# Strassen's seven products in all four feed-forwards of a decoder trunk, six direct pairs each, and the hybrid mixer's weights cut on arrival

## The chip, the cores and the metric

The kernel runs on one core of a Trainium2 chip. The metric is the device time of one execution in microseconds (us). The runs of one kernel differ by about 0.1%. One more execution is taken with the hardware profiler on; its page and its trace are what is quoted here.

## The reference, cut to what matters

The input is 512 tokens of width 1024 in float32. There are two layers; each is

```
x = x + 0.5 * ffn1(norm(x));  x = x + mixer(norm(x));  x = x + 0.5 * ffn2(norm(x))

def swiglu_ffn(x, g, w_in, w_out):            # w_in 1024 x 5632, w_out 2816 x 1024
    h = rms_norm(x, g)
    gate, up = jnp.split(h @ w_in, 2, axis=-1)
    return (jax.nn.silu(gate) * up) @ w_out
```

The mixer of layer 0 (hybrid) projects to seven parts of 512 columns: gate, q, k and v of eight retention heads, and q, k and v of eight heads of dilated window attention; the 1024 columns that come out go through an output projection. The mixer of layer 1 is stick-breaking attention with 16 heads. A last norm ends it. Everything is float32, and the kernel keeps about that accuracy on TensorE with three products for one: each operand is split into a rounded high part (hi) and the rest (lo), and hi*hi + hi*lo + lo*hi is accumulated.

## The kernel before, in words

**Data.** Activations are transposed: x is eight tiles x0 to x7 of 128 channels x 512 tokens that stay in SBUF. All large tiles come from 43 slots of 4 KB a partition. `give` (line 49) hands lists of slots to roles, and `B` (line 72) takes the next slot of a role in turn. The roles for weights are `wraw` (four slots, a weight as it comes from HBM) and `whl` (six slots, so three pairs of hi and lo). The Tile framework orders each engine's instructions from priorities and a model of their times and adds the semaphores; engines work through their queues in order. Inside mixers and the feed-forwards of `ffn_seven`, the order on TensorE is the order in the source (`ordered`, line 113).

**Weights, four ways.**

- `weight` (line 144): load raw, hi by a cast on ScalarE (line 206), lo by a subtraction on VectorE (line 207).
- `cut_ahead` (line 175) does this early, beside other work, and writes hi and lo to HBM with two transfers; `weight_cut` (line 185) later reads both, and no engine has to work on them.
- `weight_dma` (line 481): load raw, hi by a cast and minus hi by a multiplication on ScalarE (lines 485 and 486), then POOL issues a transfer that reads the weight from HBM again and adds it onto minus hi (line 487), which gives lo without VectorE.
- `centre` (line 162) is for the retention's v: the mean over each head's 64 columns is taken out on VectorE (lines 168 and 169), and the result goes to HBM.

**Feed-forwards.** There are 22 tiles of 128 gate columns and 22 of up columns. A direct pair is one of each: a tile is 8 x 3 matmuls of 512 columns (tokens). The first feed-forward of layer 0 (`ffn`, line 388) has 22 direct pairs; beside them it centres the four v weights and cuts 20 weights of the hybrid mixer ahead. The other three (`ffn_seven`, line 538) have four direct pairs and then nine quads. A quad (line 490) is two pairs done at once as a 2 x 2 product of blocks (rows are the halves of the 1024 channels, columns the two column groups; tokens are split in halves of 256) with seven products instead of eight, in Winograd's form of Strassen's method. It loads four raw blocks, makes four sums of blocks on VectorE, and cuts seven operands: four sums with `cut_form` (ScalarE and VectorE), three raw blocks with `cut_raw` (line 456, ScalarE twice and an accumulating transfer from POOL, line 461). A product is 24 matmuls of 256 columns. The other operand, seven combinations of the normed activations with hi and lo, is made once a feed-forward (`normed_forms`, line 430; lines 440 to 452), after the last direct pair in the source, and as early as VectorE comes to it. Three of the eight direct weights are cut with `weight_dma` (`BYDMA`, line 427). The quads have seven slots for raw blocks and ten for cut ones. At the end all 22 tiles of silu(gate) * up are split into hi and lo (line 580).

**Output projection.** `out_ffn` (line 300) does eight tiles of 22 x 3 matmuls in three pieces of weights each, adds half of the result to x, and makes the next norm's h (gain times x, split, line 231) and the sum of squares (line 240) for each tile as it comes. Beside it `cut_ahead` runs 12 times (first feed-forward of layer 0: eight hybrid weights, four of the stick mixer), 16 times and 16 times. The factor 1/rms (`norm_r`, line 262) is applied after the first projections.

**Hybrid mixer** (line 835). The 28 units of input weights (four gates, four each of rq, rk, dq and dk, and four each of rv and dv) are used in a fixed stream of steps. All were cut ahead; `weight_cut` takes turns between the `wraw` and the `whl` slots. First come the four gates, q and k of the first head pair and values, then steps are interleaved with the heads: scores, masks by POOL (line 777) or softmax, values. Then the output projection, whose last three chunks are done by `out_second` (line 372).

Of the kernel before, what the change touches and what calls it, by code (L numbers as in the profile page):

```python
# [20 lines left out]
P = 128  # L21
# [8 lines left out]
NORM_EPS = 1e-6  # L30
GN_EPS = 1e-5


@with_exitstack
def trunk(ctx: ExitStack, tc: tile.TileContext, a: dict, out: bass.AP):
# [17 lines left out]
    give(wraw=WSLOTS[:4], whl=WSLOTS[4:])  # L53
    home = {"h": list(range(10, 18))}

    def others():

        return [i for i in range(10, NSLOT) if i not in home["h"]]
# [116 lines left out]
    def cut_ahead(key, cols):  # L175

        hi, lo = weight(centred.get(key, array_unit(key)), cols)
        keep = dram.tile([P, 2, cols], F32, tag="cut_" + "_".join(map(str, key)), name="cut_" + "_".join(map(str, key)))
        for i, part in enumerate((hi, lo)):
            nc.sync.dma_start(keep[:, i, :], f32(part[:, :cols]))  # L180
        cut[key] = keep

    turns = [0]
# [10 lines left out]
    def unit(key, cols):  # L194
        if key in cut:
            return weight_cut(key, cols)
        return weight(array_unit(key), cols)

# [41 lines left out]
    def norm_sum(c, ss, sl=slice(0, SEQ)):  # L240
        if c == 0:
            nc.scalar.activation(out=ss[:, sl], in_=x[c][:, sl], func=AF.Square)
        else:
            s = T()[:, sl]
            nc.scalar.activation(out=s, in_=x[c][:, sl], func=AF.Square)
            nc.vector.tensor_add(out=ss[:, sl], in0=ss[:, sl], in1=s)

    def norm_chunk(c, gcol, ss):
        norm_h(c, gcol)
        norm_sum(c, ss)  # L250

# [9 lines left out]

    def norm_r(ss, epsr=None):
        ps = PS("po")
        mm(ps, ones_ms, ss, start=True, stop=True)
        r = rstd(ps, NORM_EPS, eps_n, "r")
        if epsr is not None:
            nc.vector.tensor_scalar(out=epsr, in0=ps, scalar1=NORM_EPS, scalar2=GN_EPS, op0=ALU.add, op1=ALU.mult)
        return r
# [31 lines left out]
    def out_ffn(w_out, us, gcol, ahead, n):  # L300

        ss = norm_start()
        act_set(LNEXP)
        for d in range(KC):
            ps = ACC()
            m = n * (d + 1) // KC - n * d // KC
            out_tile(w_out[d], ps, us, then=lambda p: cut_ahead(*ahead.pop(0)) if p in (8, 15)[2 - m:] else None)
            add_half(d, ps)
            norm_chunk(d, gcol, ss)
        return ss  # L310
# [61 lines left out]
    def out_second(wb, chunks, gcol):  # L372

        ss = norm_start()
        for d0 in range(0, KC, 4):
            ws = [unit((wb, d0 // 2 + i), 768) for i in range(2)]
            ps = [ATT() for _ in range(4)]
            for f in ((0, 1), (2,)):
                for i in range(4):
                    for g in f:  # L380
                        mm3(ps[i], ws[i // 2], (i % 2) * 384 + g * P, chunks[5 + g][:, 0, :], chunks[5 + g][:, 1, :],
                            g == 0, g == 2)
            for i in range(4):
                nc.vector.tensor_add(out=x[d0 + i], in0=ps[i], in1=x[d0 + i])
                norm_chunk(d0 + i, gcol, ss)
        return ss

    def ffn(r, w_in, first=None, ahead=None, extra={}):

        us = []  # L390
        give(u=others()[:FC])
        for f in range(FC):
            pg = ACC()
            if first and f == 0:
                pu = ATT()
                for k in range(KC):
                    for w, ps in zip(first, (pg, pu)):
                        mm3(ps, w, k * P, hh[k][:, 0, :], hh[k][:, 1, :], k == 0, k == KC - 1)
            else:
                proj_tile(w_in[f], pg)  # L400
            if f == 0:
                rr = r()
                act_set(SILU)
            t1 = T(tag="tp")
            nc.vector.tensor_mul(out=t1, in0=pg, in1=rr)
            s = T()
            func(s, t1, AF.Silu)
            if not (first and f == 0):
                pu = ATT()
                proj_tile(w_in[FC + f], pu)  # L410
            t2 = T(tag="tp")
            nc.vector.tensor_mul(out=t2, in0=pu, in1=rr)
            nc.vector.tensor_mul(out=t2, in0=t2, in1=s)
            u = B((P, 2, SEQ), F32R, "u")
            split(u[:, 0, :], u[:, 1, :], t2)
            us.append(u)
            if ahead and f > 1:
                if f in extra:
                    centre(extra[f])
                cut_ahead(*ahead.pop(0))  # L420
        return us

    DIRECT, FORMS_AT = 4, 3
    FIRST, BYDMA = 40, (5, 6, 7)
    HT = SEQ // 2
# [51 lines left out]

    def weight_dma(src, cols):
        raw = B((P, 1024), F32, "wraw")
        hi, lo = (B((P, 1024), F32R, "whl")[:, :cols] for _ in range(2))
        nc.sync.dma_start(raw[:, :cols], src)
        nc.scalar.copy(out=hi, in_=raw[:, :cols])
        nc.scalar.mul(out=lo, in_=f32(hi), mul=-1.0)
        nc.gpsimd.dma_start(lo, src, accum_op=ALU.add)
        return hi, lo

    def quad(wq, fm, uq):  # L490

        a21, a11, a22, a12 = (B((P, 2, SEQ), F32, "wraw") for _ in range(4))
# [12 lines left out]
        nc.vector.tensor_add(out=w75, in0=bd_, in1=s7)  # L505
        w = cut_raw(a22, wq[3])
        p2 = a22
        nc.vector.tensor_add(out=p2, in0=p1, in1=a11)
        product(bc, w, fm["T4"], False)
        w = cut_raw(a11, wq[0])  # L510
        p4 = a11
# [25 lines left out]

    def ffn_seven(ss, wd, wq, gcol, ahead=[]):

# [7 lines left out]
        for f in range(DIRECT):  # L547
            if f == 0:
                with tc.high_priority(offset=FIRST):
                    w2 = [weight(wd[i], D) for i in (0, DIRECT)]  # L550
            else:
                w2 = [weight_dma(wd[i], D) if i in BYDMA else weight(wd[i], D) for i in (f, DIRECT + f)]
            pg = ACC()
            proj_tile(None, pg, w2[0])
            if f == 0:
                rr = norm_r(ss)
                act_set(SILU)
# [3 lines left out]
            func(s, t1, AF.Silu)  # L561
            pu = ATT()
            proj_tile(None, pu, w2[1])
            t2 = T(tag="tp")
# [3 lines left out]
            nc.vector.tensor_mul(out=uqs[-1][:, f % 2, :], in0=t2, in1=s)  # L568
            if f == FORMS_AT:
                fm = normed_forms(rr, gcol, ext + late[3:])  # L570
        give(wraw=WSLOTS[:4] + ext[:3], p3=ext[3:], whl=WSLOTS[4:] + old[4:])
        for q in range((FC - DIRECT) // 2):
            uqs.append(B((P, 2, SEQ), F32, "uq"))
            quad(wq[q], fm, uqs[-1])
        order["on"] = False
        give(u=forms + ext + old[4:])
        us = []
        for f in range(FC):
            u = B((P, 2, SEQ), F32R, "u")
            split(u[:, 0, :], u[:, 1, :], uqs[f // 2][:, f % 2, :])  # L580
            us.append(u)
        give(wraw=WSLOTS[:4], whl=WSLOTS[4:])
        home["h"] = (late + old[:4])[:8]
# [251 lines left out]
    def hybrid(ss, gcol_next):  # L835
# [3 lines left out]
        for p in range(4):  # L839
            held.append(ACC())  # L840
            proj_tile(("hyb_g", p), held[-1])
            if p == 0:
# [216 lines left out]
    for c in range(KC):  # L1059
# [3 lines left out]
        if c % 2 == 0:  # L1063
            for i, (raw, _) in enumerate(first):
                sl = slice(c * P, (c + 2) * P)
                nc.sync.dma_start(raw[:, sl], a["f1_in"][i * FC][:, sl])
    for c in range(KC):
# [17 lines left out]

    hyb = [(("hyb_g", p), D) for p in range(4)]
    for n in "rd":
        for p in range(4):
            if p % 2 == 0:
                hyb += [((f"hyb_{n}v", p // 2, u), D) for u in range(2)]  # L1090
            hyb += [((f"hyb_{n}q", p), D), ((f"hyb_{n}k", p), D)]
    rv = [u for u in hyb if u[0][0] == "hyb_rv"]
    hyb = [u for u in hyb if u not in rv] + rv
    sb = []
# [5 lines left out]

    us = ffn(sums, a["f1_in"], first, hyb, {2 + 2 * i: u[0] for i, u in enumerate(rv)})
    ss = out_ffn(a["f1_out"][0], us, 8, hyb + sb[:4], 12)
    ss = hybrid(ss, 16)
    us = ffn_seven(ss, a["wd0"], a["wq0"], 16)
    ss = out_ffn(a["f2_out"][0], us, 24, sb[4:20], 16)
    us = ffn_seven(ss, a["wd1"], a["wq1"], 24)
    ss = out_ffn(a["f1_out"][1], us, 32, sb[20:], 16)
    ss = stick(ss, 40)
    us = ffn_seven(ss, a["wd2"], a["wq2"], 40)
    out_last(a["f2_out"][1], us, 48)  # L1110

# [45 lines left out]
def _layout(i):  # L1157
# [17 lines left out]
    for n, s in (("f1", "ffn1"), ("f2", "ffn2")):  # L1175
        w = g(s + "_w_out")
        o[n + "_out"] = np.stack([rows(w[l]) for l in range(2)])
    o["f1_in"] = cols(g("ffn1_w_in")[0])
    for n, w in enumerate((g("ffn2_w_in")[0], g("ffn1_w_in")[1], g("ffn2_w_in")[1])):
        c = cols(w)  # L1180
        o[f"wd{n}"] = np.concatenate([c[:4], c[FC:FC + 4]])

        c = c.reshape(2, FC, P, 2, 512)[:, 4:].reshape(2, FC // 2 - 2, 2, P, 2, 512)
        o[f"wq{n}"] = np.ascontiguousarray(c.transpose(1, 0, 4, 3, 2, 5).reshape(FC // 2 - 2, 4, P, 2, 512))
    w = g("hyb_w_in")[0]
# [51 lines left out]
```

## Time and profile before

| | |
|---|---|
| median of 3 runs | 1963.95 us (1963.61 to 1965.31) |
| the profiled execution | 1965.91 us |
| its span, first to last instruction | 1964.2 us |
| mean granted clock of TensorE | 0.994 |
| first matmul of an output projection, layer 0, first feed-forward | 251.27 us |
| bytes moved by DMA | 386.57 MB |

Times inside a profile are counted from the start of the span. Rows of waits read: engine and what it was to write, by which it was held up; us in total, how often, longest. Rows of groups read: line, engine, operation, out<-in, count | busy us, mean ns of one | idle us of the engine just before them, and what ended most of it. Rows of windows give, for each stretch, its length, then busy us of PE (matmuls), PEld (weight loads), DVE (VectorE), ACT (ScalarE) and POOL with the number of instructions, then the granted clock, the mean busy share of the 16 DMA engines, and GB/s. Rows of the chain of waits are start, duration and what. Rows of DMA issues are out<-in, issuing queue, count, size, and median us from issue to landing. q1 holds the transfers that SyncE issues, q0 those of POOL.

### The profile page before, as it was taken

The page shows a single profiled execution, that of the slowest core. Times are in us where ns is not written, and L with a number is a line of the kernel's source. Part 1 is how long each engine was busy: PE and PEld are TensorE (multiplying, and loading weights), DVE is VectorE, ACT ScalarE, POOL GpSimd, SP SyncE. Part 2 cuts the span into 40 slices and gives each one's busy share as a digit, 9 for nine tenths or more (in the row PEclk, how much of TensorE's full clock was granted, in tenths as well). Part 3 has the DMA queues.
Part 4 walks back from the last instruction along what each step waited for, and adds up shares of the span by engine and source line. Part 5 has one row for each costly group of instructions (what it writes and reads, how often), then busy time and mean ns, then how long its engine had stood idle before and what let it go on. Part 6 is the DMA issues. An engine that isn't in the chain of part 4 may idle for free.

```text
span 1964.2 us, 29107 instructions
## 1 busy us (share of the span) xinstructions
PE 1927.4 (98%) x11288; PEld 1708.9 (87%) x11288; DVE 1270.2 (65%) x1809; ACT 1002.3 (51%) x1442; POOL 145.0 (7%) x260
## 2 busy tenths in 40 slices
PE   9999999999999999999998999999999998999998
PEld 7878888888887899988778999888889878999887
DVE  7565544347767976765476677443888877677534
ACT  5344333223566566663355667343666655666523
POOL 0000000001000011100001110000222200111000
PEclk9999999999999999999999999999999999999999
DMA  7787767877533777668757766878555455777433
GB/s 245 268 290 241 257 228 251 296 254 240 177 108 104 180 172 199 161 203 295 267 173 172 199 164 151 277 245 271 162 171 159 142 146 144 199 172 170 110 91 119
DMA packets 120362, 386.57 MB, mean 197 GB/s; under 512 B 14624, under 2 KB 16288, under 8 KB 120224
## 3 DMA queue, kind: packets, MB, share of 16 engines
q1 hardware_dynamic: 107120, 337.27, 51.8%
q0 software_dynamic: 12960, 47.19, 14.0%
q8 instruction: 88, 1.44, 0.3%
q14 instruction: 50, 0.41, 0.1%
q10 hardware_dynamic: 144, 0.26, 0.0%
HBM read 296.58 MB, written 67.11 MB: 185 GB/s over the span
## 4 chain that ended last, share of the span: by engine, by line
PE 82%; DMA 7%; DVE 5%; issue 3%; ACT 2%; POOL 0%; SPq 0%; DVEq 0%; ACTq 0%; POOLq 0%
PE acc L120 42%; PE att L120 38%; PE po L120 2%; DVE whl L207 2%; DMA wraw<-f_out 1%; DMA cut_sb_k<-whl 1%; DMA whl<-wq 1%; ACT whl L206 1%; DMA wraw<-hyb_g 1%; DMA wraw<-hyb_rq 1%; DMA cut_sb_q<-whl 1%; DMA wraw<-wd 1%; DMA centred<-wraw 1%; DMA cut_sb_v<-whl 0%; PE att L123 0%
## 5 line engine op out<-in xcount | busy, mean ns | idle before, releaser
L206 ACT CAST whl<-wraw 128x1024 fp32r<-128x1024 f32 (+4 forms) x323 | 316.6, 991 | 492.3 <-PE acc L120 198.4
L207 DVE TENSOR_TENSOR whl<-wraw,whl 128x1024 fp32r<-128x1024 f32 (+4 forms) x323 | 369.7, 1151 | 303.1 <-ACT whl L206 247.4
L120 PE MATMUL acc<-u,whl 128*128 128x512 f32 (+1 forms) x2244 | 483.5, 377 | 2.0 <-DVE whl L207 2.0
L120 PEld LDWEIGHTS acc<-u,whl 128*128 128x128 f32 x2244 | 403.2, 188 | 81.0 <-DVE whl L207 3.7
L120 PE MATMUL att<-fT,whl 128*128 128x256 f32 x2592 | 324.0, 285 | 12.1 <-DMA whl<-wq 11.4
L120 PEld LDWEIGHTS att<-fT,whl 128*128 128x128 f32 x2592 | 318.6, 194 | 13.0 <-DMA whl<-wq 11.8
L120 PE MATMUL acc<-h,whl 128*128 128x512 f32 x1248 | 303.2, 393 | 6.2 <-DVE whl L207 2.9
L120 PEld LDWEIGHTS acc<-h,whl 128*128 128x128 f32 x1248 | 232.6, 188 | 60.9 <-DVE h L238 5.3
L120 PE MATMUL att<-fB,whl 128*128 128x256 f32 x1944 | 242.4, 283 | 0.0
L120 PEld LDWEIGHTS att<-fB,whl 128*128 128x128 f32 x1944 | 237.6, 192 | 0.0
L120 PE MATMUL att<-h,whl 128*128 128x512 f32 x816 | 197.7, 395 | 3.6 <-DMA whl<-wd 3.6
L120 PEld LDWEIGHTS att<-h,whl 128*128 128x128 f32 x816 | 155.1, 190 | 38.7 <-DMA whl<-wd 4.0
L459 ACT CAST whl<-wraw 128x1024 fp32r<-128x1024 f32 x81 | 84.9, 1049 | 86.3 <-PE att L120 86.3
L461 POOL DMA_DIRECT2D whl<-wq x81 | 70.1, 866 | 498.6 <-ACT whl L460 263.4
L120 PE MATMUL acc<-h,wraw 128*128 128x512 f32 x432 | 104.8, 391 | 0.0
L120 PEld LDWEIGHTS acc<-h,wraw 128*128 128x128 f32 x432 | 80.0, 188 | 16.1
L207 DVE TENSOR_TENSOR whl<-p,whl 128x1024 fp32r<-128x1024 f32 x27 | 33.1, 1225 | 88.1 <-ACT whl L206 88.1
L460 ACT ACTIVATE whl<-whl 128x1024 fp32r<-128x1024 f32 x81 | 85.9, 1060 | 2.4
L936 POOL TENSOR_SCALAR_AFFINE_SELECT t<-t 128x128 f32<-128x128 f32 x128 | 46.3, 384 | 191.3 <-DVE t L953 125.1
L102 ACT ACTIVATE t<-t 128x512 f32<-128x512 f32 (+1 forms) x91 | 51.6, 587 | 6.7 <-DVE t L789 4.2
L297 DVE SCALAR_TENSOR_TENSOR x<-acc,x 128x512 f32<-128x512 f32 (+1 forms) x34 | 22.4, 659 | 48.8 <-PE acc L120 48.7
L206 ACT CAST whl<-p 128x1024 fp32r<-128x1024 f32 x27 | 28.3, 1048 | 48.4 <-PE att L120 33.0
(183 smaller groups left out, 2146.8 us busy)
## 6 DMA issues: line engine op xcount, KB each, us to landing
wraw<-wq SPq DMA_DIRECT2D x108, 512.0 KB, 5.5
whl<-wq POOLq DMA_DIRECT2D x81, 512.0 KB, 6.6
wraw<-f_out SPq DMA_DIRECT2D x68, 448.0 KB, 4.3
wraw<-f_in SPq DMA_DIRECT2D x42, 512.0 KB, 4.7
wraw<-f_out SPq DMA_DIRECT2D x34, 512.0 KB, 4.5
wraw<-wd SPq DMA_DIRECT2D x24, 512.0 KB, 4.3
cut_sb_q<-whl SPq DMA_DIRECT2D x16, 512.0 KB, 4.4
cut_sb_k<-whl SPq DMA_DIRECT2D x16, 512.0 KB, 4.8
```

The lines of the kernel that those rows point to most:

```text
L102: r = nc.scalar.activation(out=o, in_=i, func=f, **kw)
L120: return ordered(nc.tensor.matmul(*args, **kw))
L206: nc.scalar.copy(out=hi, in_=src)
L207: nc.vector.tensor_tensor(out=lo, in0=src, in1=f32(hi), op=ALU.subtract)
L297: nc.vector.scalar_tensor_tensor(out=x[d][:, sl], in0=ps[:, sl], scalar=0.5, in1=x[d][:, sl], op0=ALU.mult, op1=ALU.add)
L459: nc.scalar.copy(out=hi, in_=raw)
L460: nc.scalar.mul(out=lo, in_=f32(hi), mul=-1.0)
L461: nc.gpsimd.dma_start(lo, src, accum_op=ALU.add)
L936: nc.gpsimd.affine_select(out=t[:, at:at + P], in_=t[:, at:at + P], pattern=[[1, P]], compare_op=ALU.is_gt, fill=0.0, base=0, channel_mult ...
```

## The change

1. **All four feed-forwards by quads.** `ffn` goes; `ffn_seven` does all four with six direct pairs and eight quads (`DIRECT = 6`). In the first, the first pair uses the weights cut at the start as before. In the others the gate and the up tile of the first pair both go ahead of the norm's matmul.
2. **First quad.** Its raw operands a22 and a11 are cut by `cut_form` (`early`); no direct weight is cut by `weight_dma` any more (`BYDMA = ()`).
3. **Slots by age.** Where roles change hands, a role's list starts with the slot used longest ago (`oldest`).
4. **Hybrid weights raw.** Nothing of the hybrid mixer is cut ahead. Its first gate weight is cut by `weight`, the other 27 units by `weight_dma`, with the `wraw` and the three pairs of `whl` slots. The four v weights are still centred ahead, now beside the first output projection.
5. **Cut ahead.** The stick mixer's 36 weights are cut beside the three output projections: 4 centrings and 12 cuts, 12 cuts, 12 cuts, spread over the first seven of the eight tiles.
6. **Norms.** The squares and sums of the last four chunks are put off to `norm_r`; in `out_second` the second half's adds and norms get a higher priority, and its three chunks of matmuls are one run for each tile.

```
-    DIRECT, FORMS_AT = 4, 3
-    FIRST, BYDMA = 40, (5, 6, 7)
+    FIRST, BYDMA = 40, ()
+DIRECT = 6
...
+    def oldest(role):
+        n = turn_of[role] % len(roles[role])
+        return roles[role][n:] + roles[role][:n]
...
+    BY_DMA = ["hyb_" + n for n in ("g", "rq", "rk", "rv", "dq", "dk", "dv")]
     def unit(key, cols):
         if key in cut:
             return weight_cut(key, cols)
-        return weight(array_unit(key), cols)
+        src = centred.get(key, array_unit(key))
+        return weight_dma(src, cols) if key[0] in BY_DMA else weight(src, cols)
...
     def norm_chunk(c, gcol, ss):
         norm_h(c, gcol)
-        norm_sum(c, ss)
+        if c < KC - 4:
+            norm_sum(c, ss)
+        else:
+            pending.append((c, ss))
     def norm_r(ss, epsr=None):
+        while pending:
+            norm_sum(*pending.pop(0))
...
     (out_ffn)
-            m = n * (d + 1) // KC - n * d // KC
-            out_tile(w_out[d], ps, us, then=lambda p: cut_ahead(*ahead.pop(0)) if p in (8, 15)[2 - m:] else None)
+            m = n * (d + 1) // (KC - 1) - n * d // (KC - 1) if d < KC - 1 else 0
+            out_tile(w_out[d], ps, us, then=lambda p: ahead.pop(0)() if p in (0, 8, 15)[3 - m:] else None)
...
     (out_second)
-            for f in ((0, 1), (2,)):
+            for f in ((0, 1), (2,)) if d0 == 0 else ((0, 1, 2),):
...
+                with tc.high_priority(offset=2 * FIRST if d0 else 0):
...
-    def quad(wq, fm, uq):
+    def quad(wq, fm, uq, early):
+        raw = (lambda t, src: cut_form(t)) if early else cut_raw
...
-        w = cut_raw(a22, wq[3])
+        w = raw(a22, wq[3])
...
-        w = cut_raw(a11, wq[0])
+        w = raw(a11, wq[0])
...
     (ffn_seven, pair f)
+            if f == 0 and first:
+                pu = ATT()
+                for k in range(KC):
+                    for w, ps in zip(first, (pg, pu)):
+                        mm3(ps, w, k * P, hh[k][:, 0, :], hh[k][:, 1, :], k == 0, k == KC - 1)
...
+            if f == 0 and first:
+                rr = rms()
+                act_set(SILU)
+            elif f == 0:
+                pu = ATT()
+                proj_tile(None, pu, w2[1])
+                rr = rms()
...
-            if f == FORMS_AT:
-                fm = normed_forms(rr, gcol, ext + late[3:])
-        give(wraw=WSLOTS[:4] + ext[:3], p3=ext[3:], whl=WSLOTS[4:] + old[4:])
+            if f == DIRECT - 1:
+                fm = normed_forms(rr, gcol, ext + late[DIRECT // 2:])
+        give(wraw=oldest("wraw") + ext[:3], p3=ext[3:], whl=oldest("whl") + old[4:])
...
     (hybrid, gate p)
-            proj_tile(("hyb_g", p), held[-1])
+            if p == 0:
+                w = weight(a["hyb_g"][0], D)
+                proj_tile(None, held[-1], w)
+            else:
+                proj_tile(("hyb_g", p), held[-1])
...
-    us = ffn(sums, a["f1_in"], first, hyb, {2 + 2 * i: u[0] for i, u in enumerate(rv)})
-    ss = out_ffn(a["f1_out"][0], us, 8, hyb + sb[:4], 12)
+    ahead = [lambda k=("hyb_rv", g, u): centre(k) for g in range(2) for u in range(2)]
+    ahead += [lambda u=u: cut_ahead(*u) for u in sb]
+    us = ffn_seven(sums, a["wd0"], a["wq0"], 0, first)
+    ss = out_ffn(a["f1_out"][0], us, 8, ahead, 16)
     ss = hybrid(ss, 16)
-    us = ffn_seven(ss, a["wd0"], a["wq0"], 16)
-    ss = out_ffn(a["f2_out"][0], us, 24, sb[4:20], 16)
+    us = ffn_seven(lambda: norm_r(ss), a["wd1"], a["wq1"], 16)
+    ss = out_ffn(a["f2_out"][0], us, 24, ahead, 12)
     (layer 1 alike, with 12)
```

More of the change, by code (lines that the diff above doesn't have):

```diff
@@ L175, in cut_ahead @@
     def cut_ahead(key, cols):
-        hi, lo = weight(centred.get(key, array_unit(key)), cols)
+        hi, lo = weight(array_unit(key), cols)
         keep = dram.tile([P, 2, cols], F32, tag="cut_" + "_".join(map(str, key)), name="cut_" + "_".join(map(str, key)))
@@ L181, in cut_ahead, with weight_dma @@
         cut[key] = keep
+    BY_DMA = ["hyb_" + n for n in ("g", "rq", "rk", "rv", "dq", "dk", "dv")]
+    def weight_dma(src, cols):
+        raw = B((P, 1024), F32, "wraw")
+        hi, lo = (B((P, 1024), F32R, "whl")[:, :cols] for _ in range(2))
+        nc.sync.dma_start(raw[:, :cols], src)
+        nc.scalar.copy(out=hi, in_=raw[:, :cols])
+        nc.scalar.mul(out=lo, in_=f32(hi), mul=-1.0)
+        nc.gpsimd.dma_start(lo, src, accum_op=ALU.add)
+        return hi, lo
     turns = [0]
@@ L246, in norm_sum @@
             nc.vector.tensor_add(out=ss[:, sl], in0=ss[:, sl], in1=s)
+    pending = []
     def norm_chunk(c, gcol, ss):
         norm_h(c, gcol)
-        norm_sum(c, ss)
+        if c < KC - 4:
+            norm_sum(c, ss)
+        else:
+            pending.append((c, ss))
     def rsqrt(b):
@@ L383, in out_second @@
             for i in range(4):
-                nc.vector.tensor_add(out=x[d0 + i], in0=ps[i], in1=x[d0 + i])
-                norm_chunk(d0 + i, gcol, ss)
-        return ss
[L388 to L421, printed above, removed]
-    DIRECT, FORMS_AT = 4, 3
-    FIRST, BYDMA = 40, (5, 6, 7)
+                with tc.high_priority(offset=2 * FIRST if d0 else 0):
+                    nc.vector.tensor_add(out=x[d0 + i], in0=ps[i], in1=x[d0 + i])
+                    norm_chunk(d0 + i, gcol, ss)
+        return ss
+    FIRST, BYDMA = 40, ()
     HT = SEQ // 2
@@ L479, in product @@
                 mm(o, l, bh, start=False, stop=k == 3, skip_group_check=True)
[L481 to L488, printed above, removed]
-    def quad(wq, fm, uq):
+    def quad(wq, fm, uq, early):
+        raw = (lambda t, src: cut_form(t)) if early else cut_raw
         a21, a11, a22, a12 = (B((P, 2, SEQ), F32, "wraw") for _ in range(4))
@@ L536, in quad, with ffn_seven @@
         put(0, x21, s1)
-    def ffn_seven(ss, wd, wq, gcol, ahead=[]):
+    def ffn_seven(rms, wd, wq, gcol, first=None):
         order["on"] = True
@@ L547, in ffn_seven @@
         for f in range(DIRECT):
-            if f == 0:
+            pg = ACC()
+            if f == 0 and first:
[4 more added lines that the diff above has]
+            elif f == 0:
                 with tc.high_priority(offset=FIRST):
                     w2 = [weight(wd[i], D) for i in (0, DIRECT)]
+                proj_tile(None, pg, w2[0])
             else:
[L552 to L556, printed above, removed]
+                w2 = [weight(wd[i], D) for i in (f, DIRECT + f)]
+                proj_tile(None, pg, w2[0])
+            if f == 0 and first:
+                rr = rms()
+                act_set(SILU)
+            elif f == 0:
+                pu = ATT()
+                proj_tile(None, pu, w2[1])
+                rr = rms()
                 act_set(SILU)
@@ L561, in ffn_seven @@
             func(s, t1, AF.Silu)
-            pu = ATT()
-            proj_tile(None, pu, w2[1])
+            if f:
+                pu = ATT()
+                proj_tile(None, pu, w2[1])
             t2 = T(tag="tp")
@@ L568, in ffn_seven @@
             nc.vector.tensor_mul(out=uqs[-1][:, f % 2, :], in0=t2, in1=s)
-            if f == FORMS_AT:
-                fm = normed_forms(rr, gcol, ext + late[3:])
-        give(wraw=WSLOTS[:4] + ext[:3], p3=ext[3:], whl=WSLOTS[4:] + old[4:])
+            if f == DIRECT - 1:
+                fm = normed_forms(rr, gcol, ext + late[DIRECT // 2:])
+        give(wraw=oldest("wraw") + ext[:3], p3=ext[3:], whl=oldest("whl") + old[4:])
         for q in range((FC - DIRECT) // 2):
             uqs.append(B((P, 2, SEQ), F32, "uq"))
-            quad(wq[q], fm, uqs[-1])
+            quad(wq[q], fm, uqs[-1], q == 0)
         order["on"] = False
-        give(u=forms + ext + old[4:])
+        ring, raws = oldest("whl"), oldest("wraw")
+        give(u=forms + [i for i in raws + ring if i not in WSLOTS] + ext[3:])
         us = []
@@ L581, in ffn_seven @@
             us.append(u)
-        give(wraw=WSLOTS[:4], whl=WSLOTS[4:])
+        give(wraw=[i for i in raws if i in WSLOTS], whl=[i for i in ring if i in WSLOTS])
         home["h"] = (late + old[:4])[:8]
@@ L1065, in trunk @@
                 sl = slice(c * P, (c + 2) * P)
-                nc.sync.dma_start(raw[:, sl], a["f1_in"][i * FC][:, sl])
+                nc.sync.dma_start(raw[:, sl], a["wd0"][i * DIRECT][:, sl])
     for c in range(KC):
@@ L1084, in sums @@
         return norm_r(ss)
[L1086 to L1093, printed above, removed]
     sb = []
@@ L1099, in trunk @@
     sb += [(("sb_oa", d), 640) for d in range(8)] + [(("sb_ob", d), 768) for d in range(4)]
-    us = ffn(sums, a["f1_in"], first, hyb, {2 + 2 * i: u[0] for i, u in enumerate(rv)})
-    ss = out_ffn(a["f1_out"][0], us, 8, hyb + sb[:4], 12)
+    ahead = [lambda k=("hyb_rv", g, u): centre(k) for g in range(2) for u in range(2)]
+    ahead += [lambda u=u: cut_ahead(*u) for u in sb]
+    us = ffn_seven(sums, a["wd0"], a["wq0"], 0, first)
+    ss = out_ffn(a["f1_out"][0], us, 8, ahead, 16)
     ss = hybrid(ss, 16)
-    us = ffn_seven(ss, a["wd0"], a["wq0"], 16)
-    ss = out_ffn(a["f2_out"][0], us, 24, sb[4:20], 16)
-    us = ffn_seven(ss, a["wd1"], a["wq1"], 24)
-    ss = out_ffn(a["f1_out"][1], us, 32, sb[20:], 16)
+    us = ffn_seven(lambda: norm_r(ss), a["wd1"], a["wq1"], 16)
+    ss = out_ffn(a["f2_out"][0], us, 24, ahead, 12)
+    us = ffn_seven(lambda: norm_r(ss), a["wd2"], a["wq2"], 24)
+    ss = out_ffn(a["f1_out"][1], us, 32, ahead, 12)
     ss = stick(ss, 40)
-    us = ffn_seven(ss, a["wd2"], a["wq2"], 40)
+    us = ffn_seven(lambda: norm_r(ss), a["wd3"], a["wq3"], 40)
     out_last(a["f2_out"][1], us, 48)
@@ L1177, in _layout @@
         o[n + "_out"] = np.stack([rows(w[l]) for l in range(2)])
[L1178 to L1184, printed above, removed]
+    nq = (FC - DIRECT) // 2
+    for n in range(4):
+        c = cols(g(("ffn1", "ffn2")[n % 2] + "_w_in")[n // 2])
+        o[f"wd{n}"] = np.concatenate([c[:DIRECT], c[FC:FC + DIRECT]])
+        c = c.reshape(2, FC, P, 2, 512)[:, DIRECT:].reshape(2, nq, 2, P, 2, 512)
+        o[f"wq{n}"] = np.ascontiguousarray(c.transpose(1, 0, 4, 3, 2, 5).reshape(nq, 4, P, 2, 512))
     w = g("hyb_w_in")[0]
```

## The prediction

> **What bounds the kernel now.** I read the page first, for the engine that is never free.
>
> ```profile
> span 1964.2 us, 29107 instructions
> PE 1927.4 (98%) x11288; PEld 1708.9 (87%) x11288; DVE 1270.2 (65%) x1809; ACT 1002.3 (51%) x1442; POOL 145.0 (7%) x260
> q1 hardware_dynamic: 107120, 337.27, 51.8%
> q0 software_dynamic: 12960, 47.19, 14.0%
> ```
>
> TensorE is busy for 98% of the span, so only two things can shorten it: less matmul time, or fewer of the remaining holes. The chain of waits, in order of time, gives the price of matmul time.
>
> ```profile
> 20.09 5.32 PE acc L120 x22
> 25.40 5.44 PE att L120 x24
> 251.27 125.12 PE acc L120 x552
> 675.71 178.58 PE att L120 x1486
> ```
>
> A tile of a direct pair is 24 matmuls of 512 columns and takes 5.44 us, so two pairs (which one quad replaces) take 4 x 5.44 = 21.76 us. A matmul of 256 columns takes 178.58/1486 = 0.1202 us; a quad has 7 products of 24, 168 x 0.1202 = 20.19 us. Seven eighths of the multiplications buy only 1.57 us a quad, 7% and not 12.5%, because a half-width matmul costs more than half.
>
> Next I read the waits of PE, and the stretches right after the longest of them.
>
> ```profile
> PE att L120 <- DMA whl<-wq: 11.4, 2, 6.0
> PE att L120 <- DMA whl<-wd: 3.6, 1, 3.6
> PEld acc L120 <- DVE h L238: 5.3, 11, 0.9
> ```
>
> ```profile
> 1010.00:1017.00 7.00, 6.18 (x15) 4.88 (x16) 6.33 (x11) 5.77 (x10) 0.86 (x1) 0.52 0.86 289
> 1041.00:1044.00 3.00, 2.92 (x13) 2.92 (x14) 0.00 (x0) 0.00 (x0) 0.00 (x0) 0.50 1.06 335
> 1652.00:1658.00 6.00, 5.22 (x24) 5.22 (x25) 0.00 (x0) 0.33 (x1) 0.00 (x0) 0.50 0.92 277
> ```
>
> Three stalls, 11.4 + 3.6 = 15.0 us, all on low parts made by accumulating transfers, all in the two feed-forwards of layer 1 between the direct pairs and the third product of the first quad. After each the granted clock is halved: 7 x 0.48 + 3 x 0.5 + 6 x 0.5 = 7.9 us more. Together 22.9 us. Their cause stands in the chain of the windows around them (start, us, what), and in the rows of the stages (PE, PEld, DVE, ACT, POOL busy, clock, DMA share, GB/s):
>
> ```profile
> 1032.27 8.77 DMA whl<-wq
> 1643.32 9.43 DMA whl<-wq
> ```
>
> ```profile
> 251.00:371.00 120.00, 120.00 (x531) 99.36 (x530) 53.87 (x58) 42.16 (x49) 1.84 (x2) 1.00 0.74 254
> 371.00:475.00 104.00, 104.00 (x570) 90.42 (x569) 51.96 (x93) 27.83 (x49) 11.30 (x22) 1.00 0.81 264
> 475.00:608.00 133.00, 132.86 (x764) 116.45 (x763) 99.12 (x218) 79.05 (x182) 5.35 (x12) 1.00 0.50 144
> 632.00:672.00 40.00, 40.00 (x175) 32.55 (x176) 37.49 (x53) 25.52 (x35) 3.60 (x4) 1.00 0.66 171
> 672.00:854.00 182.00, 181.27 (x1510) 181.07 (x1510) 131.29 (x149) 118.00 (x142) 22.46 (x26) 1.00 0.72 173
> 854.00:977.00 123.00, 120.99 (x531) 98.72 (x530) 59.96 (x65) 50.13 (x59) 0.00 (x0) 1.00 0.81 280
> ```
>
> Where the seven forms are built beside four pairs, VectorE is busy 37.49 of 40 us; everything for the first quad is late, and its accumulating transfer lands 8.8 to 9.4 us after it leaves, where two products give it 5.77.
>
> **The change, part by part.** Durations for the steps:
>
> ```profile
> L207 DVE TENSOR_TENSOR whl<-p,whl 128x1024 fp32r<-128x1024 f32 x27 | 33.1, 1225 | 88.1 <-ACT whl L206 88.1
> L206 ACT CAST whl<-p 128x1024 fp32r<-128x1024 f32 x27 | 28.3, 1048 | 48.4 <-PE att L120 33.0 <-DVE p L496 12.2 <-PE acc L120 3.2
> L440 DVE SCALAR_TENSOR_TENSOR tf<-x,gains,r 128x512 f32<-128x512 f32 x24 | 16.9, 745 | 0.0
> L207 DVE TENSOR_TENSOR fT<-tf,fT 128x512 fp32r<-128x512 f32 x24 | 15.3, 687 | 0.0
> ```
>
> *First feed-forward.* After its first pair it runs from 20.09 to 251.27, 231.2 us. The new one has five pairs (54.4) and eight quads (161.5): 215.9, so 15.3 less. The entry into the quads can add a hole; the best one of before (672 to 854) idles 0.7 of 182 us. I charge 1: **-14.3**.
>
> *Six pairs in the other three.* One quad less, two pairs more: 3 x (21.76 - 20.19) = **+4.7**.
>
> *Entry into the quads.* VectorE must do 8 x 0.745 + 22 x 0.687 = 21.1 us for the forms, 12 x 1.225 = 14.7 for weights and 18 x 0.687 = 12.4 for gates: 48 us beside 6 x 10.88 = 65.3 us of matmuls, where before it was full. The first quad's two raw operands are cut by ScalarE and VectorE, 1.05 + 1.23 = 2.3 us, inside the 5.77; two subtractions more in that quad fit, as VectorE is busy 131.29 of 182 us there. No direct weight waits for an accumulating transfer any more. I take the 22.9 as gone but for 2: **-20.9** (between -22.9 and, if one stall of 6 with its slow clock stays, -13). The slots by age change which buffer comes first; with buffers idle beforehand that is worth nothing, and if it is not, it is one of these stalls.
>
> *Norms.* The squares of the last four chunks move behind their h parts, the second half of the mixers' output goes ahead of other work, and the norm's matmul waits until both first tiles are through. What waits for h now is 5.3 us in eleven pieces; I take **-2**, between 0 and -5.3. The later norm delays the forms by one tile, 5.44 us, which the 17 us of VectorE slack cover.
>
> *Output projections.* The second one stalls now for 123 - 120.99 = 2.0 us at 16 cuts; it gets 12: **-2**. The first had 12 cuts and no hole (120.00 of 120), and gets 12 cuts and 4 centrings in seven tiles, two of them with three cuts. By the queue rows a megabyte on q1 takes 0.518 x 1964.2/337.27 = 3.02 us of all 16 engines. A tile with three cuts moves 1.44 + 3 x 1.57 = 6.2 MB, 18.6 us of transfers beside 66 x 125.12/552 = 15.0 us of matmuls. Two such tiles cost 7.3 us if nothing is evened out, 0 if all is. I take the middle: **+4**. The centrings cost VectorE two instructions each:
>
> ```profile
> L168 DVE TENSOR_REDUCE t<-wraw 128x16 f32<-128x1024 f32 x4 | 4.8, 1212 | 0.0
> L169 DVE SCALAR_TENSOR_TENSOR wraw<-t,wraw 128x1024 f32<-128x1024 f32 x4 | 4.9, 1218 | 0.0
> ```
>
> which is 9.7 us where VectorE is busy 53.87 of 120: covered.
>
> *The hybrid mixer's weights.* 27 units that came ready cut now take a cast, a negation and an accumulating transfer each. The nearest rows are the nine such weights among the direct pairs:
>
> ```profile
> L486 ACT ACTIVATE whl<-whl 128x1024 fp32r<-128x1024 f32 x9 | 9.5, 1051 | 0.1
> L485 ACT CAST whl<-wraw 128x1024 fp32r<-128x1024 f32 x9 | 9.4, 1048 | 3.5 <-PE acc L120 1.4 <-issue 1.2 <-DMA wraw<-wd 0.9
> L487 POOL DMA_DIRECT2D whl<-wd x9 | 8.0, 888 | 375.7 <-ACT whl L486 320.1 <-DVE tf L449 35.6 <-DVE tf L448 10.0
> L777 POOL TENSOR_SCALAR_AFFINE_SELECT ah<-ah 128x256 fp32r<-128x256 f32 x12 | 5.6, 481 | 57.1 <-DVE ah L207 57.1
> whl<-wd POOLq DMA_DIRECT2D x9, 512.0 KB, 6.7
> ```
>
> ScalarE gets 27 x 2.1 = 56.7 us on top of 107 in 237: a share of 0.69, no bound by itself. But the cast waits until TensorE releases one of three pairs of buffers, and behind it in ScalarE's queue stand the casts of the scores; the transfer waits for the negation on POOL, and behind it there stand the masks of L777, for which the heads wait. From release to arrival: 2.1 + 6.7, with 0.5 for the hand-overs (estimate) 9.3 us, against two tiles of 10.88 us where no attention lies between (gates, first q, k and v: eight units); against more where heads lie between. At the landings of 8.8 to 9.4 us above it is 11.4 to 12, over the limit by up to 1.1 us once a turn of three. The transfers grow too. On q0 a megabyte takes 0.14 x 1964.2/47.19 = 5.83 us, so a unit takes 0.524 x (3.02 + 5.83) = 4.64 us of all engines instead of 1.05 x 3.02 = 3.17. Some 16 units go through from 371 to 475 us, where the share is 0.81 of 104: 84 + 24 = 108 us in 104. The price lies between 0 (all hidden) and that of the nine rows, which cost one stall of 3.6 and its slow clock of 3.4: 7.0/9 x 27 = 21 us. Eight units are as exposed as those nine, 8 x 0.78 = 6.2; with 2 for the rest, **+8**.
>
> Sum: -14.3 + 4.7 - 20.9 - 2 - 2 + 4 + 8 = -22.5. The profiled execution took 1965.9, of which 1.7 lie outside the span: it would take 1943.4. The median of the runs, 1963.95, lies 2 us lower: **1941**.
>
> The Trainium skill (TensorE: Matmul & The Clock Gate, Back-to-back issue gap) gives N/2.4 + 2.5 ns for a lone matmul, 109 and 216 ns here where the rows have 120 and 227. By it a quad would gain 2.4 us, and the net five quads more about 4 us more in all. No run here reaches it, and the sum keeps the rows.
>
> **The rivals.** *The mixer's transfers fill the 16 engines* (chance 0.16). For it: 108 us asked of 104, and the stalls after transfers at shares of 0.86 to 1.06. Against: nothing waits on cut weights at 0.81. Price 22 instead of 8: 1955.
>
> *The mixer stalls long enough to lose the clock* (0.08, slower). If the landing stretches to 14 us, a turn of three pairs takes 2.1 + 14 + 0.5 - 10.88 = 6 us too long, and the three stalls above show the halved clock, 3.4 us, behind such a hole: 9.4 us in each of some five turns up to 475 us, 47 us in place of 8, so 1980. It decides from about 13 us of landing on, where the longest seen is 9.4.
>
> *The entry stalls stay and the first feed-forward gets one too* (0.06; the change would not do what its early cut is for). VectorE's queue is in order and the forms could come behind the last pair's gates. -14.3 + 9 + 4.7 + 0 - 2 - 2 + 4 + 8 = +7: 1971. Against it: 17 us of slack.
>
> *POOL's issues starve* (0.02). If each of the 27 issues had to wait out one VectorE instruction of 1.2 us, the eight exposed units would lose up to 1.2 us each, 10 us more: 1951. The row of POOL's issues, 888 ns at a VectorE 37.49/40 busy, shows no such wait. The Trainium skill (SBUF — State Buffer, SBUF: two separate sides) warns of it: VectorE's two-port instructions keep GpSimd from writing descriptors.
>
> **The numbers.** Forecast 0.68, rivals as given. About 0.2%, 3.9 us, is what a measurement of this kernel can tell from no change. Faster: 0.68 + 0.02 + 0.13 of the filled engines = 0.83; within: 0.03 of them and 0.01 of the entry stalls = 0.04; slower: 0.08 + 0.05 = 0.13. The forecast's own bounds run from -40.8 (no cost in mixer or first output projection, all waits for h and the stalls gone) upwards; I let the range reach over the filled engines to 1960, leaving out the two slow rivals.
>
> **What would show it.** Right: first output matmul at about 236 us; quads at 20.2 us each; no halved clock inside the feed-forwards; no wait of PE on wq. Wrong step by step: holes of over 1 us between 236 and 490 us released by the mixer's accumulating transfers (mixer term), DMA share at 0.95 there (first rival), halved clock there (second), a wait on the forms or on wq at a first quad (third), holes in the first output projection over 8 us. The forecast fails as a whole if the mixer takes 30 us longer than before.

## The result and the profile after

| | before | after |
|---|---|---|
| median | 1964.63 us (4 runs, 1963.61 to 1968.45) | 1933.78 us (4 runs, 1930.83 to 1934.09) |
| ratio | | 0.9836, 95% interval 0.9819 to 0.9853 |
| span of the profiled execution | 1964.2 us | 1932.4 us |

The forecast was 1941 us, range 1923 to 1960. The changed kernel is 31 us faster by the medians and 31.8 by the spans, 22.5 were forecast. First the page of the changed kernel, its totals and queues:

```profile
span 1932.4 us, 29858 instructions
PE 1910.3 (99%) x11648; PEld 1716.8 (89%) x11648; DVE 1304.9 (68%) x1854; ACT 1059.0 (55%) x1506; POOL 165.8 (9%) x285
q1 hardware_dynamic: 90992, 278.54, 44.0%
q0 software_dynamic: 16560, 60.30, 18.0%
```

There are more matmuls than before (11648 against 11288, as more of them have 256 columns), and yet PE's busy time fell from 1927.4 to 1910.3 us, by fewer multiplications and by fewer stretches at half clock. The rest of the gain is idle time. The four largest waits of PE, changed kernel:

```profile
PE acc L126 <- DMA whl<-centred: 4.3, 2, 3.2
PE att L126 <- DMA qk<-ah: 3.0, 1, 3.0
PE acc L126 <- DVE whl L225: 2.7, 3, 1.5
PE po L126 <- DVE t L1050: 1.6, 1, 1.6
```

The 15.0 us of waits on wq and wd are gone. In their place stand two on `centred` and one on the packing of the first head's k, both in the hybrid mixer. The same stages in the windows (PE, PEld, DVE, ACT, POOL busy, clock, DMA share, GB/s), changed kernel:

```profile
235.00:357.00 122.00, 120.51 (x533) 99.12 (x532) 67.19 (x72) 49.42 (x57) 2.73 (x3) 1.00 0.84 294
357.00:475.00 118.00, 110.69 (x590) 95.27 (x589) 56.10 (x98) 64.62 (x89) 25.34 (x40) 0.99 0.91 224
475.00:595.00 120.00, 120.00 (x702) 106.00 (x701) 90.42 (x204) 90.04 (x190) 13.13 (x21) 1.00 0.64 147
647.00:688.00 41.00, 41.00 (x184) 34.00 (x183) 34.90 (x47) 15.16 (x21) 0.00 (x0) 1.00 0.36 116
74.00:235.00 161.00, 161.00 (x1341) 160.83 (x1340) 119.14 (x134) 106.11 (x127) 19.16 (x22) 1.00 0.72 173
688.00:849.00 161.00, 161.00 (x1343) 161.00 (x1343) 119.00 (x135) 106.57 (x127) 19.09 (x22) 1.00 0.70 173
1036.00:1197.00 161.00, 161.00 (x1344) 161.00 (x1343) 118.70 (x134) 106.22 (x127) 19.08 (x22) 1.00 0.70 171
1638.00:1800.00 162.00, 162.00 (x1349) 161.84 (x1348) 120.42 (x135) 106.89 (x128) 19.08 (x22) 1.00 0.70 171
```

All four stretches of quads (the row from 74 us and the last three) are full: PE is busy all of it at a clock of 1.00. The only stretch with much idle time is the first half of the hybrid mixer, 110.69 of 118 us. From the times of the first matmul of each stage:

| stage | before, us | after, us | difference | forecast |
|---|---|---|---|---|
| start to first output matmul | 251.1 | 235.5 | -15.6 | -14.3 |
| first output projection | 119.7 | 121.9 | +2.2 | +4 |
| hybrid mixer | 253.9 | 263.1 | +9.2 | +8 |
| other three feed-forwards up to their output | 47.0 + 182.4, 52.5 + 188.3, 47.0 + 190.2 | 67.1 + 161.3, 66.2 + 161.3, 66.2 + 161.3 | -24.0 | -18.2 |
| second output projection | 123.0 | 120.9 | -2.1 | -2 |
| the rest | | | -1.4 | 0 |

(In the row of the three, the first number is the direct pairs, the second the quads.)

### The profile page after: what moved, and what is told of

Read it like the earlier page. It is cut to its first block, busy times and chain, and to the rows that moved or that the text cites. A ratio compares the mean times of both kernels' runs of the same rounds, so it can differ in the third digit from the quotient of the medians.

```text
span 1932.4 us, 29858 instructions
## 1 busy us (share of the span) xinstructions
PE 1910.3 (99%) x11648; PEld 1716.8 (89%) x11648; DVE 1304.9 (68%) x1854; ACT 1059.0 (55%) x1506; POOL 165.8 (9%) x285
## 4 chain that ended last, share of the span: by engine, by line
PE 94%; DMA 3%; DVE 2%; issue 1%; ACT 1%; SPq 0%; POOL 0%; DVEq 0%; ACTq 0%; POOLq 0%
PE acc L126 46%; PE att L126 45%; PE po L126 2%; DVE whl L225 1%; DMA whl<-centred 1%; PE att L129 0%; DMA cut_sb_k<-whl 0%; DMA qk<-ah 0%; DMA qk<-sp 0%; DVE h L256 0%; DMA cut_sb_v<-whl 0%; DMA wraw<-f_out 0%; ACT whl L224 0%; DMA x<-xT 0%; DMA cut_sb_q<-whl 0%
## 5 line engine op out<-in xcount | busy, mean ns | idle before, releaser
L126 PE MATMUL att<-fT,whl 128*128 128x256 f32 x3072 | 379.1, 283 | 0.0
L126 PEld LDWEIGHTS att<-fT,whl 128*128 128x128 f32 x3072 | 373.5, 192 | 0.3
L126 PE MATMUL att<-fB,whl 128*128 128x256 f32 x2304 | 287.2, 283 | 0.0
L126 PEld LDWEIGHTS att<-fB,whl 128*128 128x128 f32 x2304 | 281.2, 192 | 0.2 <-DMA whl<-wq 0.2
L126 PE MATMUL att<-h,whl 128*128 128x512 f32 x576 | 135.8, 389 | 0.0
L126 PEld LDWEIGHTS att<-h,whl 128*128 128x128 f32 x576 | 108.4, 188 | 22.6
L126 PE MATMUL acc<-whl,h 128*128 128x256 f32 x576 | 75.9, 287 | 4.3 <-DMA whl<-centred 4.3
L126 PEld LDWEIGHTS acc<-whl,h 128*128 128x128 f32 x576 | 73.4, 194 | 5.8 <-DMA whl<-centred 4.7
L225 DVE TENSOR_TENSOR u<-uq,u 128x512 fp32r<-128x512 f32 x88 | 58.9, 688 | 13.4 <-ACT u L224 12.8
L224 ACT CAST u<-uq 128x512 fp32r<-128x512 f32 x88 | 52.6, 617 | 17.3 <-PE att L126 10.3
```

The source lines that it names most:

```text
L126: return ordered(nc.tensor.matmul(*args, **kw))
L224: nc.scalar.copy(out=hi, in_=src)
L225: nc.vector.tensor_tensor(out=lo, in0=src, in1=f32(hi), op=ALU.subtract)
```

## The experiments

Where only one execution was taken, its span and the lengths of its stages are set against those of the changed kernel, 1932.4 us. The kernel before, run beside the experiments, had spans from 1960.0 to 1966.0 us, more than the 0.1% of its first three runs. So a few us of span in a single execution prove little, and the waits and the lengths of stages carry the argument. A hole is a stretch in which PE stands idle and waits.

### The hybrid mixer: ready weights

```
-        return weight_dma(src, cols) if key[0] in BY_DMA else weight(src, cols)
+        return weight_ready(cols) if key[0] in BY_DMA else weight(src, cols)
```

> Leaves out the cutting of the hybrid mixer's 28 input weights: hi and lo are read ready from HBM (from stick weights that are cut there, so the mixer's numbers mean nothing), two transfers each, no ScalarE, VectorE or POOL work. Between the first gate matmul and the first direct matmul of the next feed-forward lie 263.1 us in the changed kernel and 253.9 in the one before. Theory (the accumulating transfers make the mixer's three holes): 254 us, whole run about 1924. Rival (the mixer is longer for another part of the change, the slots or the order): 260 us or more.

Measured: span 1923.4 us, mixer 253.5. The mixer has no hole over 0.5 us left. So the 9.2 us come from how the weights are cut, and not from the order of the steps. This kernel also takes its pairs of buffers from both lists of slots; that the slots alone do no harm is shown by the next kernels, which keep them and lose the holes.

### All weights of the mixer by VectorE, or rv alone

```
-    BY_DMA = ["hyb_" + n for n in ("g", "rq", "rk", "rv", "dq", "dk", "dv")]
+    BY_DMA = []
```

> All 28 hybrid weights are cut on arrival by ScalarE and VectorE, with no accumulating transfer. Theory (landing time and full DMA engines make the holes): VectorE gets 27 x 1.22 = 33 us more and has room, the mixer takes 254 to 257 us. Rival (VectorE is the bound among the heads, where it is busy 70 to 90 per cent): holes of 0.5 to 2 us at the heads, mixer 263 us or more.

Measured: span 1924.5, mixer 255.4. There is one hole in the mixer, 1.3 us at 526 us, behind VectorE among the dilated heads.

```
+    BY_DMA = ["hyb_" + n for n in ("g", "rq", "rk", "dq", "dk", "dv")]
```

> Only the four rv units are cut by ScalarE and VectorE, the other 23 by accumulating transfers as in the changed kernel. Theory (the holes stand where two pairs are held by values and the third has to land in time): the holes at the values go, mixer 255 to 258 us. Rival (all 16 engines are full, whichever weight it is): the holes move to the next units, mixer 261 us or more.

Measured: span 1926.7, mixer 258.7, 0.7 above the theory's range. The two holes at the values are gone, but a third stays, 3.5 us long with 3.4 us of halved clock at its end:

```profile
PE att L126 <- DMA qk<-ah: 3.5, 1, 3.5
```

It isn't a weight at all. It is the packing of the first head's k, a move within SBUF that runs beside the weights' transfers. The windows of the changed kernel's first two holes, the piece of its chain of waits that ends the second, and its landing times say why:

```profile
394.00:398.00 4.00, 0.84 (x7) 0.64 (x6) 0.94 (x2) 0.63 (x1) 0.73 (x1) 1.00 1.06 261
402.00:406.00 4.00, 0.95 (x8) 0.82 (x7) 0.48 (x1) 0.27 (x1) 0.00 (x0) 1.00 0.93 238
```

```profile
396.14 8.25 DMA qk<-ah
```

```profile
whl<-centred POOLq DMA_DIRECT2D x4, 512.0 KB, 9.4
whl<-hyb_g POOLq DMA_DIRECT2D x3, 512.0 KB, 6.9
qk<-ah SPq DMA_DIRECT2D x32, 128.0 KB, 6.5
```

The same row in the kernel before:

```profile
qk<-ah SPq DMA_DIRECT2D x32, 128.0 KB, 2.4
```

The 16 DMA engines are busy nearly all the time there. The accumulating transfers of the values take 9.4 us to land, where the nine among the direct weights of the kernel before took 6.7. The packings, 32 in the mixer, take 6.5 instead of 2.4 at the median, and those of the first head's k took 8.25 us, where a landing within 6 us of their issue would have left no hole. So both accounts hold: late weights make two holes and full engines the third. That the full engines also lengthen the first two is argued from the landing times, not tested by itself.

### Half and half

```
+    BY_DMA = ["hyb_" + n for n in ("dq", "dk", "dv")]
```

> Hybrid gates, rq, rk and rv cut by ScalarE and VectorE, dq, dk and dv by accumulating transfers. Theory (transfers limit the mixer up to about 475 us, VectorE and ScalarE only among the heads after it): no hole over 0.5 us in the mixer, about 254 us, 9 us less than the changed kernel. Rival (the limit is VectorE in the retention heads): holes there, 257 us or more.

Measured: median 1923.91 us, ratio to the kernel before 0.9797 (0.9782 to 0.9812), mixer 253.9, no hole over 0.5 us. The same stretch in this kernel, where DMA is busy 0.65 and not 0.91:

```profile
357.00:475.00 118.00, 117.80 (x635) 101.73 (x634) 79.91 (x127) 55.55 (x83) 16.41 (x30) 1.00 0.65 176
```

The changed kernel itself, on the same chip:

> The changed kernel as it is, on the chip of the three kernels beside it, as their measure: 1931 to 1934 us; mixer 263.1 us with three holes (3.3, 3.2, 1.3) at the same places.

Measured: median 1933.56 us, ratio 0.9845 (0.9831 to 0.9860), mixer 264.0, holes 2.9, 1.5 and 2.3 us. The intervals of the half and half kernel and of the changed one lie apart: half and half is faster, by 9.7 us of median.

### The early cuts spread evenly

```
-    ss = out_ffn(a["f1_out"][0], us, 8, ahead, 16)
+    ss = out_ffn(a["f1_out"][0], us, 8, ahead, 14)
```

and 13 and 13 for the other two, on top of half and half.

> The same, and the 40 early steps spread 14, 13, 13 over the three output projections instead of 16, 12, 12. Theory (two tiles with three cuts cost the first projection its 1.6 us hole): hole at 340 us gone, first projection 119.7 to 120.5 us, 1 to 2 us less than the kernel with 16, 12, 12. Rival (the hole is the last tile's, whatever is spread): unchanged within 0.5 us.

Measured: median 1924.67 us, ratio 0.9801 (0.9784 to 0.9817). The theory fell: the hole at 341 us went, one of 1.6 us came at 317, and the second projection got one of 1.8 us at 906; the first projection took 121.7 us, as in the half and half kernel. With two cuts in a tile as with three, there are holes. The windows of these two, and the transfer in the chain of waits before each:

```profile
316.00:319.00 3.00, 1.43 (x7) 0.84 (x6) 2.93 (x5) 1.68 (x3) 0.00 (x0) 1.00 1.01 336
905.00:908.00 3.00, 1.21 (x6) 0.67 (x4) 2.98 (x4) 1.33 (x2) 0.00 (x0) 1.00 0.94 319
```

```profile
308.39 5.33 DMA cut_sb_k<-whl
896.97 5.40 DMA cut_sb_q<-whl
```

VectorE is busy all through them (2.93 and 2.98 of 3 us), but it comes late to this work: before the first, ScalarE had stood idle for 7.0 us and VectorE for 3.7 us until the write of a cut weight to HBM had landed. That write holds the pair of buffers that the next weight needs, and both chains run back to one.

The same spread with all hybrid weights cut by ScalarE and VectorE:

> All hybrid weights by ScalarE and VectorE, early steps 14, 13, 13. Theory: as the kernel with all by VectorE, its one hole of 1.4 us among the dilated heads stays; within 2 us of the half and half one, slightly longer.

Measured: median 1927.70 us, ratio 0.9818 (0.9804 to 0.9833), 3.0 us above the half and half kernel with the same spread. That is more than the 2 us expected, though the two intervals overlap. The hole of 1.3 us among the dilated heads is still there; the first projection takes 120.8 us.

### Four pairs

```
-DIRECT = 6
+DIRECT = 4
```

> Four direct pairs and nine quads in all feed-forwards, everything else as changed. Matmul time alone falls by 4 x 1.57 = 6.3 us. Theory (the entry needs VectorE's room beside six pairs: 48 us of work there, 39 beside 43.5 us of matmuls with four): holes of 3 to 10 us before the first quads, run 5 to 35 us longer than the changed kernel. Rival (the early cut and the direct weights without accumulating transfers had already cured the entry): holes under 1 us, run about 6 us shorter, 1927.

Measured: span 1958.0 us, 25.6 longer, though its matmul time is shorter. Its waits, and the window of the first four pairs:

```profile
PE att L126 <- ACT whl L224: 9.9, 4, 4.2
PE acc L126 <- DMA whl<-centred: 6.2, 2, 3.4
PE att L126 <- DVE whl L225: 5.4, 4, 1.5
```

```profile
20.00:56.00 36.00, 32.10 (x142) 26.27 (x140) 35.14 (x52) 19.09 (x28) 0.00 (x0) 0.99 0.42 141
```

The first and the third row, 15.3 us, are the four entries into the quads: the first quad's first operand waits for its cut, which is late because VectorE is full, 35.14 of 36 us; the chain of waits into the first entry runs through VectorE's work on the forms. With the early cut alone the entry isn't cured.

### The early cut undone

```
-            quad(wq[q], fm, uqs[-1], q == 0)
+            quad(wq[q], fm, uqs[-1], False)
```

> The first quad's raw operands go by accumulating transfers again, six pairs kept. Theory (the transfer needs about 9 us from its buffer's release, two products give 5.8): a hole of 3 to 6 us at the third product of each first quad, most with the halved clock, 4 x 5 to 4 x 9 us longer. Rival (six pairs alone give VectorE and the transfers enough lead): no hole, run within 1 us of the changed kernel.

Measured: span 1962.9, 30.5 longer. The waits of this kernel, and the first of its four entries:

```profile
PE att L126 <- DMA whl<-wq: 23.0, 4, 6.6
```

```profile
79.00:91.00 12.00, 5.39 (x33) 5.19 (x32) 2.11 (x3) 2.50 (x3) 0.86 (x1) 0.72 0.97 270
```

Each first quad waits at its third product, 6.6, 5.5, 6.1 and 4.8 us. In each case the clock falls to half before the hole is over and stays there for 6.8 us; the four stretches of quads take 169.7, 168.9, 169.0 and 168.4 us instead of 161.3. Room on VectorE doesn't help here. That the operand's pair of buffers is released only by the last direct tile, so that the transfer can't leave earlier, is read from the code.

### The norms as before

```
-        if c < KC - 4:
-            norm_sum(c, ss)
-        else:
-            pending.append((c, ss))
+        norm_sum(c, ss)
```

with the other parts of point 6 undone as well, and the norm's matmul between the first two tiles.

> The norms as before the change: squares at once, no priority for the second half of the mixers' output, norm's matmul between the first two tiles. Theory (these parts removed waits for h of 1.5 to 2.6 us at each mixer's end and 1 us at the start of layer 1): 4 to 6 us longer than the changed kernel. Rival (the waits went because nothing is cut beside the last output tile): within 1.5 us of it.

Measured: span 1942.2, 9.8 longer, twice the theory. The norm's own matmul now waits for the sum of squares, 2.9 us at 627 and 3.8 us at 1581 us, and from the second hole on the clock is halved for 6.8 us:

```profile
PE po L126 <- DVE ss L264: 6.7, 2, 3.8
```

```profile
1580.00:1592.00 12.00, 8.17 (x23) 5.55 (x23) 8.12 (x12) 5.39 (x7) 0.00 (x0) 0.72 0.31 102
```

The profile of the kernel before shows no matmul that waits for the sums. Why the old order waits for them in the new kernel stays open.

### Slots in fixed order

```
-        n = turn_of[role] % len(roles[role])
+        n = 0
```

> The lists of slots in fixed order instead of by age. Theory (the buffers lie idle beforehand): within 1 us of the changed kernel. Rival (an operand of the first quad, or the first output weights, would wait for a slot still in use): holes of 2 to 6 us at the entry or the end of the quads.

Measured: span 1965.6 us, 33.2 longer; the theory fell, the rival holds. Its waits, and the windows after the quads of the first and the second feed-forward:

```profile
PE acc L126 <- DVE whl L225: 15.5, 6, 4.9
PE acc L126 <- ACT whl L224: 4.8, 4, 1.6
```

```profile
237.00:249.00 12.00, 7.10 (x19) 5.28 (x19) 9.50 (x12) 3.12 (x5) 0.00 (x0) 0.57 0.35 115
864.00:873.00 9.00, 5.77 (x14) 4.29 (x15) 5.09 (x8) 3.77 (x6) 0.00 (x0) 0.62 0.20 58
```

TensorE stops between the last quad and the output projection (1.1 to 1.6 us, then 2.8 to 4.9 more) in all four feed-forwards, and the clock is halved from the second of these holes on. The cause follows from counting in the code, and the waits agree. A quad takes 14 of the ten cut slots in turn. Nine quads take 126, and six are left over, so the fixed list begins with the pair that the third product from the end used. Eight quads take 112, two are left over, and the list begins with the pair of the very last product. The first output weight can't be cut before the quads are done, and its subtraction then stands behind other work of VectorE (9.50 of 12 us busy). The second feed-forward's entry got two holes as well, 1.4 and 1.9 us; that the mixer leaves the turns at another place is the likely reason, not shown.

### The first feed-forward direct

```
-    us = ffn_seven(sums, a["wd0"], a["wq0"], 0, first)
+    us = ffn_seven(sums, a["wd0"], a["wd0"], 0, first, FC)
```

with 22 direct pairs laid out for it and no quads.

> The first feed-forward with 22 direct pairs and nothing cut beside it; the rest is the changed kernel. Theory (a quad saves 1.57 us of matmul time, and 2.2 us of the gain came from holes of the cutting): 21 pairs x 10.88 = 228.5 us after the first pair, first output matmul at about 248 us instead of 235.5, whole run 12 to 14 us longer than the changed kernel. Rival (most of the gain came from taking the cutting away): first output matmul at 240 us or earlier, run at most 5 us longer.

Measured: span 1943.8, 11.4 longer, 0.6 under the theory's range; first output matmul at 248.0 us against 235.5, as the theory had it. The quads are worth 12.5 us there, and 3.1 of the 15.6 come from taking the early cuts away.

## Why the prediction was right, and where its sizes were off

**Price of matmul time: right.** The quads' rate, 0.1202 us a matmul of 256 columns, is 161.3/1344 = 0.1200 now, and eight quads, forecast at 161.5, take 161.3 us in all four feed-forwards. The first feed-forward came 1.3 us under the forecast, because the charge of 1 us for its entry wasn't needed.

**Entry into the quads: right, a little too careful.** The 22.9 us were forecast to go but for 2. They went: nine quads of 168 matmuls at 0.120 us are 181.4 us, and took 188.3 and 190.2 in layer 1, so 6.9 and 8.7 were lost in them; eight are 161.3 and took 161.3. The third stall, on a direct weight, is gone too. The reasons hold: six pairs for VectorE (four cost 25.6 us) and the early cut for the transfer (its removal costs 30.5). But VectorE's slack was smaller than the 17 us forecast, as the 48 us of work left some out: from 620 to 688 us it is busy 58.99 of 68 us, and in the first feed-forward 48.73 of 54.

**Slots by age: wrong.** The step that failed is "with buffers idle beforehand that is worth nothing, and if it is not, it is one of these stalls". The buffers weren't idle, and the stall was not one of the old ones: it stands at the other end of the quads and arises only because there are eight of them. The fixed order costs 33 us. In the sum the term was 0 and stayed 0, as the change carries its own remedy.

**Norms: mis-sized.** Forecast -2. What the direct stages lost beyond the two added pairs (21.76 us) and the old stalls is 1.7 us in layer 0, about 1 and 2.6 in layer 1, together about 5. The row behind the forecast's bound, 5.3 us in eleven pieces, is of weight loads (PEld). The matmuls themselves waited less for h in the kernel before:

```profile
PE acc L120 <- DVE h L238: 1.7, 4, 0.6
PE acc L120 <- ACT h L237: 1.4, 2, 1.2
```

Of these 3.1 us, 0.2 are left. Another 1.0 us at 978 us was a wait on a weight's low part, no part of the norms, and is gone as well; the last us or so isn't traced. Undone in the new kernel, point 6 costs 9.8, mostly by the wait for the sum of squares, which was not in the sum.

**First output projection: mis-sized.** Forecast +4, measured +2.2. The sum priced the load of the engines in tiles with three cuts. The even spread has no such tile and is no shorter, so that was not the right price; in the even spread the holes come behind writes of cut weights that hold their buffers.

**The hybrid mixer: right in place and size, in part by luck.** Forecast +8, measured +9.2: holes at 394, 402 and 441 us, the first 100 us of the mixer, of 3.2, 3.0 and 1.1 us, and one halved clock of 3.4 us that costs about 1.7, the half of it. The forecast charged eight exposed units alike, and of these only values stalled, 4.3 us. The other half, 3.0 and the slow clock behind it, comes from the packing of k, which was no term of the sum. The rival of filled engines was true as a mechanism (a share of 0.91 in that stretch, 108 us asked of 104 by the estimate) and small in price. The slower rival was half true: the clock was lost once, but its 14 us of landing were not reached; the values' 9.4 was the worst kind, and the longest single landing there was 10.2. POOL's issues did not starve: its 27 in the mixer took 0.86 to 0.88 us each, where the row before has 0.89.

What is left between -22.5 and -31.8: 5.8 in the entries and norms of the three feed-forwards, 1.8 in the first output projection, 1.3 in the first feed-forward, 1.4 in stages that were forecast unchanged, less 1.2 in the mixer.

## What to carry to other kernels

A saving in operations has to be priced by the measured rate of the smaller instructions: an eighth fewer multiplications gave 7% here. The matmuls gave about 12.5 - 4.8 = 8 us in all; the other 24 came from holes, and the slow clock behind them, that left with the change. When buffers are dealt out in turn, changing the number of turns changes which buffer comes next, so order them by their last use wherever a list changes hands. Choose between an engine and a transfer for the same work stage by stage: where DMA is full, a subtraction on VectorE is the cheaper way, and half and half had the shortest mixer of the kernels that really cut its weights, 253.9 us, as long as with all weights cut ahead.

## What the runs showed of the hardware

Short holes can lose the clock and longer ones keep it. In the changed kernel a hole of 3.2 us at 394 us left the clock at 1.00, and the one of 3.0 us at 402 was followed by 3.4 us at half. In its second profile it was the other way round: the clock was lost at the first hole (2.9 us) and at the third (2.3 us). In the kernel with four pairs a hole of 1.9 us and, two matmuls later, one of 1.3 us were followed by 3.4 us at half in three feed-forwards. In the four holes of the kernel without the early cut the clock fell 2.4 to 3.3 us after the hole began. The Trainium skill (TensorE: Matmul & The Clock Gate, What's actually happening) says that the gate watches windows of about 3.4 us that run freely; the halved stretches here, 3.4 and 6.8 us long, agree with that.

A packing of 128 KB within SBUF takes longer where the DMA engines are full. Those of k in the changed kernel took 5.0 to 8.2 us to land (medians of groups of two to four) when the engines' share in the 4 us from their issue was 0.97 or more. In the kernel before, at shares of 0.56 to 0.93, they took 2.2 to 3.7 us.
